# Storing sums of squares as rows, and the tail's results without a step's delay, in a hybrid attention encoder layer

## The chip, the cores and the metric

The kernel runs on one core of a Trainium2 chip. The metric is the device time in microseconds. The profiled execution is one more run of the same program, recorded by the hardware profiler.

## The reference

One layer of a bidirectional encoder is applied to two request groups of 2048 tokens each, with model width 1024, in float32. Both share one set of weights:

```python
h = rms_norm(x, norm_w)
proj = h @ w_in          # [q_a 512 | k_a 128 | v_a 128 | g_a 512 | q_b 512 | k_b 512 | v_b 512 | g_b 512]
...
o_a = windowed_gqa_sink(q_a, k_a, v_a, sink_a) * jax.nn.silu(g_a)
...
o_b = neighbourhood_attn(q_b, k_b, v_b, rpb_b) * jax.nn.silu(g_b)
x = x + jnp.concatenate([o_a, o_b], axis=-1) @ w_out
gate = jax.nn.sigmoid(x @ w_ple_gate)
return x + (p @ w_ple) * gate
```

Group A is attention within 128 tokens on either side, 8 query heads over 2 key heads, with normalised and partly rotated q and k and a learned sink. Group B is attention over a grid 64 tokens wide, in windows of 8 by 16, with a learned relative bias. `rms_norm` divides each row by the root of its mean square: the kernel works these means out once per row and uses them in both groups. The last two lines are the layer's tail: `p @ w_ple`, 256 inputs wide, can be computed at any time, since it needs nothing of the attention.

## The kernel before, in words

Matrices are held as a high and a low part, and each product is three matmuls of TensorE (PE). A sequence of 2048 rows is cut into NT = 16 blocks of 128. The stages follow each other in one stream:

- Stage A, f = 0 to 31, one step for each block of both sequences: `proj_a(f)` projects into pk, pq and pg (keys and values, queries, gate), while the two attention units of an earlier block run between its matmuls, at shares of the step that a table (PLAN_A) gives. In an attention unit, pt are transposes of the weights pr, po is the product with vv, and `fin` copies po with ACT (L738), adds with DVE (L741), multiplies by the gate pgt with DVE (L742) into ot and stores ot (L743, oa_d).
- Stage B, f = 32 to 95, the same for group B in two halves of the heads: the matmuls are pqk and pvg, with weight blocks wa and wb that are loaded when a half begins (L192).
- `ple_ahead(n)` computes `p @ w_ple` for n = 0 to 7, 512 columns each, in eight results m = 0 to 7 (pple, six matmuls each). Five of them (AHEAD) run inside the stream beside the last attention units, and n = 5, 6, 7 run as the tail behind it. ACT copies each result into a tile ev (L1007), and SP stores that to ple_d[n] (ple_d_327, 328 and 329 are those of n = 5, 6 and 7), from where it is read at the very end.
- The output projection and the gate's product, in seven products a step (acca, accc), each with operands opd that ACT and DVE split from loaded blocks raw (L1158, L1160), combined weights s (L1140) and residual blocks xres (L1245).

All large DMAs are issued by SyncE (SP), in order. A scheduler orders the instructions of each engine by when their inputs and buffers are free; those in `P(...)` or `pinned(...)` keep the order of the program. PSUM has three sets of buffers: "pj" with 3, "sc" with 3 and "ms" with 2; po, pqt (transposes of q) and the small transposes share "ms". In the tail, ev has five buffers (tag "s", SB = 5).

The means of squares of block f stand in column f of ms_a, one per partition. Stage B needs them in another order, as rows of the grid, in ms_b. So `proj_a` stores each column to DRAM:

```python
P(nc.sync.dma_start(ms_d[128 * f:128 * f + 128].rearrange("(p c) -> p c", c=1), ms))
```

This is L601: 128 pieces of one number. After the last block of a sequence (t == NT-1, so f = 15 and 31) `regroup(s)` lists the 16 reads of ms_b from ms_d (L639), which are issued two at a time from then on, and `stats_b(s)` works on ms_b later. Loads of the next rows are stn (normalised path, L338, read by ACT's squares at L369) and stx.

In `ple_ahead`, a store is put on a list and asked for when the next result has been copied, so always one result later:

```python
P(nc.scalar.copy(ev, ps))
store_ple(1)
made.append((ple_d[n][:, m], ev))
```

`load_coming()` asks for the next of eight weight blocks that the output product needs (wb, L976).

Of the kernel before, what the change touches and what calls it, by code (L numbers as in the profile page):

```python
# [11 lines left out]
F32 = mybir.dt.float32  # L12
# [5 lines left out]
SEQ = 2048  # L18
DM = 1024
NT = SEQ // 128  # L20
# [80 lines left out]
def emit(ctx, tc, io):  # L101
    nc = tc.nc
# [4 lines left out]
    def ptile(shape, tag, name):  # L107
        tag = PSM.get(tag, tag)
        return pp.tile(shape, F32, tag=tag, name=name, bufs=PSB[tag])
# [8 lines left out]
    ms_a = cp.tile([128, 2 * NT], F32, tag="ms_a", name="ms_a")  # L118
# [11 lines left out]
    ms_d = dram.tile([2 * SEQ], F32, tag="ms_d", name="ms_d")  # L130
# [28 lines left out]
    P = tc.keep_in_program_order  # L159
# [6 lines left out]
    def flush(key):  # L166
        pump(max((i + 1 for i, (k, _) in enumerate(jobs) if k == key), default=0))
# [72 lines left out]
    def pinned(ins):  # L240

        if last_pe:
            tc.add_manual_dep(ins.ins, last_pe.pop().name,
                              mybir.DependencyInfo(mybir.DependencyClass.NoSync, mybir.DependencyReason.DATA),
                              reason="tensor engine order")
        last_pe.append(ins.ins)
# [7 lines left out]
    def mm(out, lhsT, rhs, start, stop):  # L254
        pinned(nc.tensor.matmul(out, lhsT, rhs, start=start, stop=stop))  # L255

    def tr(out, in_, eye=ident):
        pinned(nc.tensor.transpose(out, in_, eye))  # L258
# [63 lines left out]
    ap = ab_stack.enter_context(tc.tile_pool(name="ab", bufs=1))  # L322
# [60 lines left out]
    ps = ptile([128, 512], "ms", "pwarm")  # L383
# [82 lines left out]
    for i in range(2):  # L466
        t = ap.tile([128, 2, 512], F32R, tag=f"q2{i}", name=f"q2{i}")
# [24 lines left out]
    def proj_a(f):  # L492
        s, t = divmod(f, NT)
# [68 lines left out]
        sq = ap.tile([128, 512], F32, tag="sq", name="sq", bufs=2)  # L562
# [35 lines left out]
        else:  # L598
            gate()
        held[f] = q, gs, y  # L600
        P(nc.sync.dma_start(ms_d[128 * f:128 * f + 128].rearrange("(p c) -> p c", c=1), ms))  # L601
        if t == NT - 1:
            regroup(s)
        else:
            regroup_next()
# [23 lines left out]
    def regroup(s):  # L629
        rows = ms_d.rearrange("(r k c) -> r k c", k=4, c=16)  # L630
        regroups.extend((ms_b[:, i:i + 1], rows[8 * (i // 4):8 * (i // 4) + 8, i % 4, :].rearrange("r c -> c r"))
                        for i in range(NT * s, NT * s + NT))
# [3 lines left out]
    def regroup_next():  # L636

        for dst, src in regroups[:2]:
            P(nc.sync.dma_start(dst, src))  # L639
        del regroups[:2]  # L640
# [293 lines left out]
    ple_d = [dram.tile([128, KT, TW], F32, tag=f"ple_d{n}", name=f"ple_d{n}") for n in range(len(tiles))]  # L934
    p_st, p_rs, early = {}, {}, {}

    def load_p(n):
        if n < len(tiles):
            s, u = tiles[n]
            p_st[n] = []  # L940
            for k in range(2):
                st = main.tile([128, TW], F32, tag="stage", name="p32", bufs=2)
                nc.sync.dma_start(st, io["p_t"][s][128 * k:128 * k + 128, TW * u:TW * u + TW])
                p_st[n].append(st)

    def split_p(n, later=False):

        t = p_rs[n] = main.tile([128, 2, 2, TW], F32R, tag="xr", name="p_r", bufs=2)

        def job(hi, lo, src):  # L950
            nc.scalar.copy(hi, src)
            nc.vector.tensor_tensor(out=lo, in0=src, in1=hi.bitcast(F32), op=ALU.subtract)
        for k, src in enumerate(p_st.pop(n)):
            todo = partial(job, t[:, k, 0], t[:, k, 1], src)
            if later:
                jobs.append((f"p{n}", todo))
            else:
                todo()
# [13 lines left out]
    def load_coming(n=1):  # L972

        for name, tag, key in coming[:n]:
            w = main.tile([128, 2, 512], F32R, tag=tag, name=tag, bufs=1)
            nc.sync.dma_start(w.bitcast(F32), parts_d[key])  # L976
            early[name].append(w)
        del coming[:n]

    made = []  # L980

    def store_ple(n):

        for dst, ev in made[:n]:
            nc.sync.dma_start(dst, ev)
        del made[:n]

    def ple_ahead(n, tail=False):

        load_p(n + 1)  # L990
        for m in range(KT):
            if m % 4 == 3 and (n < 3 or m == 3):
                load_coming()
            ps = ptile([128, TW], "pj", "pple")
            if m == 5 and n + 1 < len(tiles):
                split_p(n + 1)
            flush("p0")
            for k in range(2):
                w, c = early["p"][2 * (m // 4) + k], 128 * (m % 4)
                for i, (a, b) in enumerate(((0, 0), (0, 1), (1, 0))):  # L1000
                    mm(ps, w[:, a, c:c + 128], p_rs[n][:, k, b], k == 0 and i == 0, k == 1 and i == 2)
                    yield 215
            if tail:
                ev = main.tile([128, TW], F32, tag="s", name="ev", bufs=SB)
            else:
                ev = ap.tile([128, TW], F32, tag=("ev", "sq")[m // 2 % 2], name="ev", bufs=3 - m // 2 % 2)
            P(nc.scalar.copy(ev, ps))  # L1007
            store_ple(1)
            made.append((ple_d[n][:, m], ev))

    qs = {}

# [4 lines left out]
    def filler(f):  # L1017

        gen = proj_a(f) if f < 2 * NT else proj_b(f)
        for n, (cost, last_one) in enumerate(gen):  # L1020
            if last_one:
                next(gen)
            elif hold[0] > 0:
                hold[0] -= 1
            elif n % step[0] == step[0] - 1:
                pump()
            yield cost

    def drain(gen, count=10 ** 9):
        for _ in range(count):  # L1030
            if next(gen, None) is None:
                return
# [16 lines left out]
    def paired(f, n):  # L1049
# [20 lines left out]
        else:  # L1070
            for name in ("a12", "a22"):
                load_early(name)
        w_b[half] = w

    stream = chain(*(paired(f, last[f]) if f in last else filler(f) for f in range(2, 6 * NT) if f - 1 not in last),
                   *(ple_ahead(n) for n in range(AHEAD)))
    drain(stream, 24)
    done = 2
# [32 lines left out]
                keys_b(*p)  # L1111
            owed = 16
    drain(stream)
    store_ple(1)


    ab_stack.close()
    with tc.tile_pool(name="c", bufs=1, reuse_waits="tile") as op:
# [171 lines left out]

        load_raw(0, 0)
        drain(ple_ahead(AHEAD, True))
        load_raw(0, 1)
        drain(ple_ahead(AHEAD + 1, True))
        for _ in range(4):
            load_x()
# [5 lines left out]
            piece(0, k)  # L1302
        load_q(0, "s2")
        drain(rest)
        store_ple(1)
        for _ in range(4):
            load_x()
        for name in ("s1", "s3", "s4"):
# [1 line left out]
        for m in range(7 * len(groups)):  # L1310
            n, i = divmod(m, 7)
# [92 lines left out]
```

## Time and profile before

| | |
|---|---|
| time, median of 3 runs | 2491.75 us (2488.02 to 2493.52) |
| profiled execution | 2489.69 us, span 2487.9 us, mean granted TensorE clock 0.997 |
| busy time in the span | PE 2459.3, PEld 2078.0, DVE 1702.9, ACT 1413.9, POOL 863.4 us |
| ms_d stores | 32, of 0.5 KB each, in 128 pieces |
| HBM traffic | 308.24 MB read, 133.19 MB written, 177 GB/s over the span |

PE is TensorE's matmuls, PEld its weight loads (beside the matmuls), DVE the vector engine, ACT the scalar engine, POOL GpSimd and SPq the DMA queue of SyncE. An engine's row counts its own work, not its waits. The granted clock is TensorE's, 1.00 being full speed.

### The profile page before, as it was taken

How to read it: one execution, taken by the hardware profiler on the slowest of the kernel's cores; microseconds unless marked ns; L12 is line 12 of the kernel's file. 1: busy time of each engine (PE TensorE's matmuls, PEld its weight loads, DVE VectorE, ACT ScalarE, POOL GpSimd, SP SyncE). 2: the span in 40 equal slices, each digit the busy share in tenths (PEclk: the TensorE clock that was granted, in tenths of full speed). 3: DMA queues.
4: the chain of work that ended last, by engine and by line, in shares of the span. 5: the costliest groups of instructions: out<-in, count | busy, mean ns of one | idle time of the engine just before them, and what ended most of it. 6: DMA issues, size and time to landing. Idle time of an engine off the chain costs nothing.

```text
span 2487.9 us, 40537 instructions
## 1 busy us (share of the span) xinstructions
PE 2459.3 (99%) x13048; PEld 2078.0 (84%) x13048; DVE 1702.9 (68%) x4210; ACT 1413.9 (57%) x3405; POOL 863.4 (35%) x1365
## 2 busy tenths in 40 slices
PE   9999999999999999999999999999999999999999
PEld 7888888888878888888788888888777888888887
DVE  6777777777765666666666666666536655687776
ACT  6777776777664665565656566666653222344443
POOL 5555555555444544544444444443100000000000
PEclk9999999999999999999999999999999999999999
DMA  7655554455374566555855566667876445756765
GB/s 204 143 111 96 98 88 102 96 92 98 82 195 137 167 190 183 169 167 184 288 171 184 177 205 210 199 198 239 295 255 233 161 169 175 267 171 219 243 227 169
DMA packets 247140, 438.87 MB, mean 176 GB/s; under 512 B 32400, under 2 KB 86800, under 8 KB 241680
## 3 DMA queue, kind: packets, MB, share of 16 engines
q1 hardware_dynamic: 246640, 436.27, 59.6%
q8 instruction: 104, 1.70, 0.3%
q14 instruction: 108, 0.88, 0.1%
q10 hardware_dynamic: 288, 0.01, 0.0%
HBM read 308.24 MB, written 133.19 MB: 177 GB/s over the span
## 4 chain that ended last, share of the span: by engine, by line
PE 91%; DMA 4%; DVE 3%; ACT 1%; issue 1%; POOL 0%; SPq 0%; ACTq 0%; DVEq 0%; POOLq 0%
PE pqk L255 14%; PE acca L1226 14%; PE pvg L255 14%; PE accc L1226 10%; PE pg L255 6%; PE pq L255 5%; PE scb L255 4%; PE ptb L258 3%; PE pob L255 3%; PE pple L255 3%; PE pk L255 3%; PE po L255 3%; PE sc L255 3%; PE pt L258 2%; DMA stn<-x_n 1%; DMA vw<-v_d 1%
## 5 line engine op out<-in xcount | busy, mean ns | idle before, releaser
L287 ACT ACTIVATE s<-s,nm 128x320 f32<-128x320 f32 (+6 forms) x512 | 294.4, 576 | 314.9 <-DVE nm L282 193.9
L255 PE MATMUL pvg<-wb,xr 128*128 128x512 f32 x1536 | 462.6, 408 | 1.3 <-DMA wb<-sp_0wb 0.6
L255 PE MATMUL pqk<-wa,xr 128*128 128x512 f32 x1536 | 442.9, 410 | 0.0
L255 PEld LDWEIGHTS pqk<-wa,xr 128*128 128x128 f32 x1536 | 266.1, 189 | 36.9
L255 PEld LDWEIGHTS pvg<-wb,xr 128*128 128x128 f32 x1536 | 266.7, 189 | 34.2 <-DMA wb<-sp_0wb 2.2
L1208 ACT CAST opd<-raw 128x512 fp32r<-128x512 f32 x224 | 131.5, 618 | 273.3 <-PE acca L1226 115.2
L356 POOL TENSOR_TENSOR xr<-stx,xr 128x512 fp32r<-128x512 f32 x188 | 241.6, 1295 | 106.3 <-ACT xr L355 84.0
L1209 DVE TENSOR_TENSOR opd<-raw,opd 128x512 fp32r<-128x512 f32 x224 | 146.4, 685 | 151.7 <-ACT opd L1208 151.7
L255 PE MATMUL pg<-wb,xr 128*128 128x512 f32 x768 | 233.5, 410 | 1.8 <-DVE vv L518 1.0
L255 PE MATMUL pq<-wa,xr 128*128 128x512 f32 x768 | 219.4, 400 | 0.0
L271 DVE CUSTOM_DVE_ANT_0 s<-scb,bias 128x288 f32<-128x288 f32 (+3 forms) x256 | 142.0, 555 | 104.6 <-PE scb L255 104.5
L137 POOL TENSOR_TENSOR yb<-vrb,power 128x8 f32<-128x8 f32 x64 | 106.5, 1664 | 236.1 <-DVE vrb L787 222.6
L1226 PE MATMUL accc<-opd,wb 128*128 128x512 f32 x768 | 176.7, 389 | 0.0
L1226 PE MATMUL acca<-opd,wa 128*128 128x512 f32 x768 | 176.6, 391 | 0.0
L1226 PE MATMUL acca<-opd,s 128*128 128x512 f32 x768 | 175.4, 389 | 0.0
L1226 PEld LDWEIGHTS acca<-opd,wa 128*128 128x128 f32 x768 | 145.1, 189 | 30.3
L1226 PEld LDWEIGHTS accc<-opd,wb 128*128 128x128 f32 x768 | 144.2, 188 | 29.9
L1226 PEld LDWEIGHTS acca<-opd,s 128*128 128x128 f32 x768 | 144.2, 188 | 29.9
L918 DVE TENSOR_TENSOR otb<-pob,otb 64x512 f32<-64x512 f32 x128 | 88.1, 689 | 112.8 <-ACT otb L917 111.2
L255 PEld LDWEIGHTS pob<-p_t,vw 128*128 128x128 f32 (+2 forms) x832 | 133.0, 189 | 27.6 <-DVE p_t L899 5.0
L255 PEld LDWEIGHTS pq<-wa,xr 128*128 128x128 f32 x768 | 135.1, 189 | 17.3
L715 DVE TENSOR_TENSOR pr<-pt,pr 128x512 fp32r<-128x512 f32 (+2 forms) x248 | 135.5, 549 | 16.5 <-ACT pr L713 13.2
(167 smaller groups left out, 5177.0 us busy)
## 6 DMA issues: line engine op xcount, KB each, us to landing
stx<-x_b SPq DMA_DIRECT2D x128, 256.0 KB
vw<-v_d SPq DMA_DIRECT2D x112, 256.0 KB
stx<-x_a SPq DMA_DIRECT2D x64, 256.0 KB
stn<-x_n SPq DMA_DIRECT2D x64, 256.0 KB
v_d<-vb SPq DMA_DIRECT2D x64, 256.0 KB
ple_d<-ev SPq DMA_DIRECT2D x64, 256.0 KB
xres<-x_r SPq DMA_DIRECT2D x64, 256.0 KB
x_d<-r SPq DMA_DIRECT2D x64, 256.0 KB
```

The lines of the kernel that those rows point to most:

```text
L137: nc.gpsimd.tensor_tensor(out=y, in0=v, in1=power.broadcast_to([128, n]), op=ALU.pow)
L255: pinned(nc.tensor.matmul(out, lhsT, rhs, start=start, stop=stop))
L258: pinned(nc.tensor.transpose(out, in_, eye))
L271: nc.vector.tensor_tensor_reduce(out=s, in0=ps[:, :n], in1=bias, scale=1.0, scalar=-3.0e38, op0=ALU.add, op1=ALU.max, accum_out=sm["mx"][: ...
L287: ex = nc.scalar.activation(ss[i], ss[i], AF.Exp, bias=nm[:, i:i + 1], accum_out=den[:, i:i + 1])
L356: low.tensor_tensor(out=lo, in0=raw, in1=hi.bitcast(F32), op=ALU.subtract)
L715: nc.vector.tensor_tensor(out=pr[r, 1, to], in0=pt[r, c], in1=pr[r, 0, to].bitcast(F32), op=ALU.subtract)
L918: nc.vector.tensor_tensor(out=ot[a:a + 64], in0=pq[a:a + 64], in1=ot[a:a + 64], op=ALU.add)
L1208: P(nc.scalar.copy(hi, v))
L1209: P(nc.vector.tensor_tensor(out=lo, in0=v, in1=hi.bitcast(F32), op=ALU.subtract))
L1226: pinned(nc.tensor.matmul(ps, w[k][:, a, c:c + 128], o[:, b], start=i in (0, 1, 4) and k == 0 and j == 0, stop=k == 3 and j == 2, skip_gro ...
```

## The change

It has three parts.

1. The 32 stores of ms_d columns are gone. At f = 15 and f = 31, after pg's matmuls and the gate, PE transposes the sequence's 16 columns of ms_a into a PSUM tile pms (tag "ms", 16 x 128), ACT copies it to a tile row, and SP stores 16 rows of 128 numbers, 512 bytes each, in one DMA.
2. `ple_ahead` asks for one of the eight weight blocks per n, at m == 3, instead of two at n = 0, 1, 2 and one at n = 3, 4.
3. In the tail (n = 5, 6, 7) a result's store is asked for right after its copy, and the two `store_ple(1)` that stored what was left on the list are gone.

```diff
--- before.py
+++ after.py
@@ -598,8 +598,12 @@
         else:
             gate()
         held[f] = q, gs, y
-        P(nc.sync.dma_start(ms_d[128 * f:128 * f + 128].rearrange("(p c) -> p c", c=1), ms))
         if t == NT - 1:
+            ps = ptile([128, 512], "ms", "pms")
+            tr(ps[:NT, :128], ms_a[:, NT * s:NT * s + NT])
+            row = ap.tile([128, 512], F32, tag="sq", name="row", bufs=2)
+            P(nc.scalar.copy(row[:NT, :128], ps[:NT, :128]))
+            P(nc.sync.dma_start(ms_d[s * SEQ:(s + 1) * SEQ].rearrange("(t p) -> t p", p=128), row[:NT, :128]))
             regroup(s)
         else:
             regroup_next()
@@ -989,7 +993,7 @@
 
         load_p(n + 1)
         for m in range(KT):
-            if m % 4 == 3 and (n < 3 or m == 3):
+            if m == 3:
                 load_coming()
             ps = ptile([128, TW], "pj", "pple")
             if m == 5 and n + 1 < len(tiles):
@@ -1006,7 +1010,10 @@
                 ev = ap.tile([128, TW], F32, tag=("ev", "sq")[m // 2 % 2], name="ev", bufs=3 - m // 2 % 2)
             P(nc.scalar.copy(ev, ps))
             store_ple(1)
-            made.append((ple_d[n][:, m], ev))
+            if tail:
+                nc.sync.dma_start(ple_d[n][:, m], ev)
+            else:
+                made.append((ple_d[n][:, m], ev))
 
     qs = {}
 
@@ -1111,7 +1118,6 @@
                 keys_b(*p)
             owed = 16
     drain(stream)
-    store_ple(1)
 
 
     ab_stack.close()
@@ -1302,7 +1308,6 @@
             piece(0, k)
         load_q(0, "s2")
         drain(rest)
-        store_ple(1)
         for _ in range(4):
             load_x()
         for name in ("s1", "s3", "s4"):
```

PE at the end of stage A (f = 31), where pg's last matmuls are followed by stage B's first (pqk) and by the transposes of the gate (pgt) and of q (pqt); before:

```order
2815 L255 MATMUL pg<-wb_120,xr 128x512 x3
2816 L255 MATMUL pqk<-wa_9639,xr 128x512 [waits DMAHW0_49]
2817 L255 MATMUL po<-pr,vv 128x512 [waits Activation_49]
2818 L255 MATMUL po<-pr,vv 128x512
2819 L255 MATMUL pqk<-wa_9639,xr 128x512
2820 L255 MATMUL pqk<-wa_9639,xr 128x512 [waits Pool_49]
2821 L255 MATMUL pqk<-wa_9641,xr 128x512 [waits DMAHW1_49]
2822 L255 MATMUL pqk<-wa_9641,xr 128x512
2823 L258 MATMUL pgt<-ident,g_9740 128x128 [waits DVE_49]
2824 L258 MATMUL pgt<-ident,g_9740 128x128
2825 L258 MATMUL pqt<-ident,q 128x2x64 [waits PE_49]
```

and now:

```order
2816 L255 MATMUL pg<-wb_120,xr 128x512 x3
2817 L258 MATMUL pms<-ident,ms_a 16x128 [waits PE_49]
2818 L255 MATMUL pqk<-wa_9614,xr 128x512 [waits DMAHW3_49]
2819 L255 MATMUL po<-pr,vv 128x512 [waits Activation_49]
2820 L255 MATMUL po<-pr,vv 128x512
2821 L255 MATMUL pqk<-wa_9614,xr 128x512
2822 L255 MATMUL pqk<-wa_9614,xr 128x512 [waits Pool_49]
2823 L255 MATMUL pqk<-wa_9616,xr 128x512 [waits DMAHW4_49]
2824 L255 MATMUL pqk<-wa_9616,xr 128x512
2825 L258 MATMUL pgt<-ident,g_9715 128x128 [waits DVE_49]
2826 L258 MATMUL pgt<-ident,g_9715 128x128
2827 L258 MATMUL pqt<-ident,q 128x2x64 [waits Activation_49]
```

One transpose of ms_a stands behind pg, and pqt waits for ACT where it waited for PE itself. At f = 15 the same transpose stands between the last pg and the first pk of f = 16, and waits for DVE, PE and ACT.

SP at the same place; wb are the weight blocks of stage B's first half, stx rows of x, oa_d group A's results. Before:

```order
242 L743 DMA oa_d_84<-ot 128x2x128
243 L601 DMA ms_d<-ms_a 128x1
244 L192 DMA wb_9859<-sp_0wb_188 128x1024
245 L338 DMA stx<-x_b 128x512 x2
246 L601 DMA ms_d<-ms_a 128x1
247 L192 DMA wb_9861<-sp_0wb_189 128x1024
248 L192 DMA wb_9863<-sp_0wb_190 128x1024
249 L192 DMA wb_9865<-sp_0wb_191 128x1024
250 L192 DMA wb_9867<-sp_0wb_192 128x1024
251 L192 DMA wb_9869<-sp_0wb_193 128x1024
252 L192 DMA wb_9871<-sp_0wb_194 128x1024
253 L192 DMA wb_9873<-sp_0wb_195 128x1024
```

and now:

```order
215 L747 DMA oa_d_84<-ot 128x2x128
216 L192 DMA wb_9837<-sp_0wb_188 128x1024
217 L338 DMA stx<-x_b 128x512 x2
218 L192 DMA wb_9839<-sp_0wb_189 128x1024
219 L192 DMA wb_9841<-sp_0wb_190 128x1024
220 L192 DMA wb_9843<-sp_0wb_191 128x1024
221 L192 DMA wb_9845<-sp_0wb_192 128x1024
222 L192 DMA wb_9847<-sp_0wb_193 128x1024
223 L606 DMA ms_d<-row 16x128
224 L192 DMA wb_9849<-sp_0wb_194 128x1024
225 L192 DMA wb_9851<-sp_0wb_195 128x1024
226 L643 DMA ms_b<-ms_d 128x1x1 x2
```

The two stores of one column are gone, one store of 16 rows stands ahead of the last two wb, and the reads of ms_b follow it.

SP in the tail, where the stores of n = 6 (ple_d_328) and n = 7 (ple_d_329) meet the loads of the output product. Before:

```order
889 L985 DMA ple_d_328<-ev 128x512 x7
890 L1245 DMA xres<-x_r 128x512 x4
891 L1158 DMA raw<-oa_d_83 128x4x512
892 L1160 DMA raw<-ob_d_85 128x2048
893 L985 DMA ple_d_328<-ev 128x512
894 L985 DMA ple_d_329<-ev 128x512 x2
895 L1140 DMA s_23454<-sums_228 128x512
896 L1140 DMA s_23456<-sums_228 128x512
897 L1140 DMA s_23458<-sums_228 128x512
898 L1140 DMA s_23460<-sums_228 128x512
899 L985 DMA ple_d_329<-ev 128x512 x6
900 L1245 DMA xres<-x_r 128x512 x4
```

and now:

```order
860 L1014 DMA ple_d_328<-ev 128x512 x6
861 L1146 DMA s_23433<-sums_228 128x512
862 L1014 DMA ple_d_328<-ev 128x512
863 L1146 DMA s_23435<-sums_228 128x512
864 L1014 DMA ple_d_328<-ev 128x512
865 L1251 DMA xres<-x_r 128x512 x4
866 L1164 DMA raw<-oa_d_83 128x4x512
867 L1166 DMA raw<-ob_d_85 128x2048
868 L1014 DMA ple_d_329<-ev 128x512 x3
869 L1146 DMA s_23437<-sums_228 128x512
870 L1146 DMA s_23439<-sums_228 128x512
871 L1014 DMA ple_d_329<-ev 128x512 x5
```

The last store of n = 6 has moved ahead of the loads xres and raw, and two of the four s loads stand further up. The eight loads of part 2 stand between the same neighbours in both.

## The prediction

> **What bounds the kernel now.** I read the page first, then the waits of PE, a table of windows round the longest of them, the timelines of the queue and engines there, and the chain that ended last.
>
> ```profile
> span 2487.9 us, 40537 instructions
> ...
> PE 2459.3 (99%) x13048; PEld 2078.0 (84%) x13048; DVE 1702.9 (68%) x4210; ACT 1413.9 (57%) x3405; POOL 863.4 (35%) x1365
> ```
>
> PE is busy for 2459.3 of 2487.9 us. The change takes no matmul away, so it can win only idle PE time, plus time in which PE ran at half clock. The waits of PE (engine, tile and line that waited, releaser; us in total, times, longest) say where the idle time lies:
>
> ```profile
> PE pple L255 <- ACT ev L1007: 5.7, 1, 5.7
> PE pt L258 <- DVE ot L742: 5.4, 2, 4.9
> ...
> PE pvg L255 <- DMA wb<-sp_0wb: 0.6, 2, 0.3
> ```
>
> Two single waits stand out, 5.7 us in the tail and 4.9 us at the end of group A's projections. The windows (stretch; length, then busy time of PE, PEld, DVE, ACT, POOL; granted clock, DMA share, GB/s) cover both:
>
> ```profile
> 667.00:674.00 7.00, 7.00 (x43) 6.00 (x42) 2.84 (x13) 2.39 (x9) 4.58 (x13) 1.00 0.50 20
> 674.00:679.00 5.00, 0.47 (x5) 0.26 (x3) 1.23 (x4) 3.30 (x10) 0.00 (x0) 0.98 0.51 172
> 679.00:682.00 3.00, 2.65 (x13) 2.65 (x14) 2.88 (x7) 2.05 (x5) 0.00 (x0) 0.50 0.21 68
> 704.00:713.00 9.00, 9.00 (x52) 7.77 (x51) 6.16 (x18) 5.17 (x15) 4.52 (x7) 1.00 0.95 44
> 1770.00:1774.40 4.40, 2.50 (x14) 1.72 (x13) 1.53 (x4) 1.94 (x5) 1.15 (x3) 1.00 1.07 314
> 1774.50:1777.80 3.30, 3.30 (x11) 2.73 (x10) 0.91 (x2) 1.47 (x3) 0.00 (x0) 0.50 0.96 358
> 1862.50:1868.50 6.00, 0.37 (x2) 0.00 (x0) 1.39 (x2) 0.59 (x2) 0.00 (x0) 0.84 1.02 399
> 1868.50:1873.40 4.90, 4.85 (x11) 3.80 (x12) 0.00 (x0) 1.87 (x4) 0.00 (x0) 0.50 0.99 378
> ```
>
> Each idle stretch is followed by a stretch at granted clock 0.50: 2.65 us of PE work after the first, 4.85 us after the second. The DMA column differs between the two places: in the tail the queues move 399 GB/s and are full, at 667 they are half busy and move 20 GB/s.
>
> **Part 1, the sums of squares.** What stands in SP's queue before that slow stretch is a per-block store of 128 single numbers, then the load of the next block's rows, stn:
>
> ```profile
> 662.75 0.80 SPq L601 DMA_DIRECT2D ms_d<-ms_a  x1
> ...
> 666.34 1.58 SPq L338 DMA_DIRECT2D stn<-x_n  x2
> ```
>
> The chain that ended last has that load, and one of the same kind early on, beside a load of the same shape (stx) that had no such store ahead of it (start, duration, what):
>
> ```profile
> 38.99 2.72 DMA stx<-x_a
> ...
> 43.75 9.09 DMA stn<-x_n
> ...
> 666.34 9.18 DMA stn<-x_n
> ```
>
> A clean landing takes 2.72 us, one behind the store 9.18 us. Then ACT, in order, waits with its squares for stn, and everything queued behind it waits too, among it the copy that PE's transposes need:
>
> ```profile
> 675.60 0.63 ACT L369 ACTIVATE stn<-stn 128x512 f32<-128x512 f32 x1 [4.92 <-DMA stn<-x_n]
> ```
> ```profile
> 679.35 0.69 PE L258 MATMUL pt<-ident,s 128*128 128x128 f32 x2 [4.88 <-DVE ot L742]
> ```
>
> ACT was free at 675.60 − 4.92 = 670.68. With a clean landing stn is there at 666.34 + 1.58 + 2.72 = 670.6 at the latest, so ACT starts 4.92 us sooner and PE's transposes come at 679.35 − 4.92 = 674.43, just where PE's idle time began (679.35 − 4.88 = 674.47). The stall goes whole: 4.88 us. The half-clock stretch behind it goes with it: half of 2.65, 1.3 us. The windows have a second clogged place, 704 to 713: share 0.95 at 44 GB/s with the last two of these stores in the queue ahead of the eight weight blocks wb. The two waits of pvg for wb, 0.6 us, are put down to it. Other late stn loads on the chain (43.75) left no long wait of their own on PE; they are taken at nothing. Gain: 4.88 + 1.3 + 0.6 = 6.8 us.
>
> The Trainium skill, "DMA: Bandwidth & Descriptors", section "Anatomy of one DMA — SWDGE (gpsimd) path", gives a transfer a fixed cost of about 2.0 us and then its bytes; by that alone a store of 512 bytes would have been gone at 664.8 and would hold nothing, and this part would win nothing, as in rival (b). The same page's "Specifications" say that pieces under 512 bytes cost a read-modify-write, which agrees with the 20 GB/s and speaks the other way.
>
> What is added are two transposes on PE, two small ACT copies, and two stores of 16 rows in the place of 32. The transpose of f=15 needs the PSUM buffer of po, which DVE gives back with the second of these:
>
> ```profile
> 348.97 0.86 DVE L741 TENSOR_TENSOR ot<-po,ot 64x256 f32<-64x256 f32 x2 [2.17 <-ACT ot L738]
> ```
> ```profile
> 349.28 1.37 PE L255 MATMUL pk<-wx,xr 128*128 128x256 f32 x10
> ```
>
> It stands on PE ahead of these matmuls, so PE waits from 349.28 to 349.83: 0.6 us, and the matmuls of pk and all of the next block stand behind it. At f=31 the new transpose itself finds its buffer free, but the four transposes of q behind it now take the same buffer after the row's copy, which comes on ACT after the gate's tanh:
>
> ```profile
> 713.45 0.69 ACT L592 ACTIVATE gs<-pg,y 128x512 f32<-128x512 f32 x1
> ```
> ```profile
> 713.55 0.60 PE L258 MATMUL pqt<-ident,q 128*128 128x128 f32 x4
> ```
>
> No row of before copies 16x128. It lies between a 128x4 and a 128x128 operation of ACT:
>
> ```profile
> 713.23 0.19 ACT L293 ACTIVATE es<-es 128x4 f32<-128x4 f32 x1
> ```
> ```profile
> 665.04 0.28 ACT L506 ACTIVATE sq<-pk 128x128 f32<-128x128 f32 x1
> ```
>
> I take the latter, as it is the nearer in width. tanh ends at 714.14, the copy at 714.42, so PE waits 0.9 to 1.0 us instead of starting at 713.55. Cost: 0.6 + 1.0 = 1.6 us, from 0 (if the work behind catches up at a later wait) to 1.6 plus a half-clock stretch for each (below). On SP the row's store of f=31 waits for that copy too, until about 714.5, with the last two wb blocks, two loads of ms_b and an oa_d store queued behind it; the wb blocks overwrite what pg's matmuls read until about 713, and with the clog gone they land before pvg wants them. Part 1 together: −6.8 + 1.6 = −5.2 us.
>
> **Part 2, the weight blocks.** In program order the eight loads are spread over eight row blocks instead of five. The order of SP's queue has them between the same neighbours as before, since the scheduler places them by when their buffers come free. Nothing removed, nothing added: 0 us. The clock loss at 1774 (rows above) stays, as it follows waits for vw.
>
> **Part 3, the tail's stores.** Before, each result's store was asked for one product later, so the last one of 328 stood behind the loads for the output products:
>
> ```profile
> 1853.29 3.30 SPq L1245 DMA_DIRECT2D xres<-x_r  x4
> 1856.64 0.43 SPq L1158 DMA_DIRECT2D raw<-oa_d  x1
> 1857.12 0.50 SPq L1160 DMA_DIRECT2D raw<-ob_d  x1
> 1857.72 2.05 SPq L985 DMA_DIRECT2D ple_d<-ev  x3
> ```
>
> Its data had been ready since 1853.41 + 0.59 = 1854.0:
>
> ```profile
> 1853.41 0.59 ACT L1007 COPY ev<-pple 128x512 f32<-128x512 f32 x1 [0.55 <-PE pple L255]
> ```
>
> The chain and the two engines show what the place cost: the store landed 10.09 us after its issue, ACT's next copy waited for that ev buffer, and PE for the copy.
>
> ```profile
> 1857.72 10.09 DMA ple_d<-ev
> ```
> ```profile
> 1867.91 1.56 ACT L1007 COPY ev<-pple 128x512 f32<-128x512 f32 x3 [7.25 <-DMA ple_d<-ev]
> ```
> ```profile
> 1868.55 2.93 PE L255 MATMUL pple<-p_r,wa 128*128 128x512 f32 x6 [5.68 <-ACT ev L1007]
> 1871.28 2.32 PE L1226 MATMUL acca<-opd,wa 128*128 128x512 f32 x5
> ```
>
> After, this store is issued at once, ahead of those 3 MB, and can land before the copy wants its buffer (1867.91 − 7.25 = 1860.7), even at several times the clean 2.72 us. PE then runs its last product without the 5.68 us, and the 4.85 us of work at clock 0.50 shrink by half, 2.4 us. Late next is the following ev buffer: its store now goes out behind the raws and lands at about 1867, but what needs the PSUM behind it is only the third accumulator of the output product, since the first two sit in other buffers; so I take nothing for it. The loads pushed back by one store lose under 1 us of a full queue, and the operands' splitting has the time that the last 5.68 us gave back. Gain: 5.68 + 2.4 = 8.1 us.
>
> **The sum.** −5.2 + 0 − 8.1 = −13.3 us. The profiled execution took 2489.69 us (1.8 us beyond its span), which gives 2476.4. It lies 2.06 us under the median of the three runs (2488.02 to 2493.52); the mean of all four times is 2490.75, and from there the forecast is 2477.4 us.
>
> **Rivals.** (a) Only part 1 wins. The tail's queue is full (399 GB/s at 1862 to 1868), so the wait moves to the next ev buffer or to the output product's operands and is paid in the same size. Against it is the buffer order above; for it, that the same bytes have to pass. Time: 2490.75 − 5.2 = 2485.5. (b) Only part 3 wins. What holds stn may not be the 4-byte store: half a KB could be gone well inside the 2.72 us that a clean load of 256 KB takes, that is before 666.34, and then stn is late for another reason that the change leaves as it is. For it, the slow stretch lasts to 674, over 11 us after the store's issue; against it, the clean load and the late ones differ in nothing else that the trace shows. The costs of the two transposes stay: 2490.75 + 1.6 − 8.1 = 2484.2. (c) Slower: the two new waits of PE come on PE's path at 349 and 713, and each also trips the clock, while (a) and (b) both fail. In the windows 1.9 us of idle PE time within 4.40 us (1770) was followed by 3.30 us at 0.50, a loss of 1.65 us; it decides from about that much idle time in one such stretch, and the new waits are put at 0.6 and 1.0. Price 1.6 + 2 × 1.65 = 4.9: 2495.6. The Trainium skill, "TensorE: Matmul & The Clock Gate", Part 1's table of the two states, has the clock drop only after an idle window of about 3.4 us, by which (c) would cost 1.6 us at most; the 1770 row, where it dropped after 1.9 us of scattered idleness, differs from that. (d) Both wins are nothing and the costs hidden: 2490.8, for instance if the stall at 674 returns because the next load is late and the tail is bound by bytes.
>
> **How the numbers follow.** Both parts win 0.62 (2477.4), (a) 0.12, (b) 0.12, (c) 0.07, (d) 0.07. A measurement of this kernel tells about 0.2%, 5 us, from no change. (a) and (b) lie near that edge and are split two to one: faster 0.62 + 0.16 = 0.78, within 0.2% 0.08 + 0.07 = 0.15, slower 0.07. The lower end takes the new costs as hidden (−1.6), and the best of the runs shown (2488.02, 2.7 under the mean) with some of the late early loads won as well: 2471. The upper end reaches over (a) and (b) to 2487; (c) and (d) are left out.
>
> **What would show it.** In the profile after: PE's wait of pt for ot at 674 gone and no clock of 0.50 at 679; stn landing in about 3 us; a small PE wait at pk of f=16 and at pqt of f=31; no ACT wait of 7 us for ple_d at 1860 and no PE wait at pple. A wait of acca or accc in the first 15 us of the output products would speak for (a), a slow stn with no ms_d store ahead of it for (b), a clock of 0.50 at 350 or 715 for (c). The forecast is wrong if the time does not fall by more than 5 us.

## The result, and the profile after

The change took 2474.14 us (median of six runs, 2473.60 to 2477.33) where the kernel before took 2492.64 us (median of six, 2488.02 to 2497.40): a ratio of 0.9928, 95% interval 0.9915 to 0.9941, that is 18 us less, 15 to 21. The profiled pair went from 2489.69 to 2477.33 us, 12.4 us less. The kernel before spreads more from run to run than the change does; what that means for the sum comes below.

The page of the change, its first part:

```profile
span 2475.5 us, 40506 instructions
...
PE 2455.8 (99%) x13050; PEld 2074.9 (84%) x13050; DVE 1704.6 (69%) x4210; ACT 1413.6 (57%) x3407; POOL 863.3 (35%) x1365
```

PE's busy time fell by 3.5 us and its idle time by 8.9 us. Of the two waits of PE (us in total, times, longest) that headed the table before, that of pple for ev is gone, and that of pt for ot is down from 5.4 us to 0.6. The longest is now the wait of group B's product (pob) for its loaded values vw, ahead of the tail. It was 2.6 us in all before, and neither part 1 nor part 3 touches it. Two small new ones belong to the added transposes:

```profile
PE pob L255 <- DMA vw<-v_d: 4.2, 4, 2.6
...
PE pqt L258 <- ACT row L605: 0.5, 1, 0.5
PE pms L258 <- DVE ot L745: 0.5, 1, 0.5
```

At the end of stage A, SP's timeline has no ms_d store ahead of stn. The second of the two stn loads stands in the chain that ended last, with 4.37 us where the first of them had 9.18 before. That is more than the 2.72 us of a clean load, but ACT's squares start without a wait for it:

```profile
662.76 0.38 SPq L747 DMA_DIRECT2D oa_d<-ot  x1
666.77 1.59 SPq L338 DMA_DIRECT2D stn<-x_n  x2
```
```profile
668.03 4.37 DMA stn<-x_n
```
```profile
671.03 0.62 ACT L369 ACTIVATE stn<-stn 128x512 f32<-128x512 f32 x1
```

The windows answer to those of before (length; busy PE, PEld, DVE, ACT, POOL; granted clock, DMA share, GB/s):

```profile
667.00:674.00 7.00, 7.00 (x42) 5.98 (x40) 3.44 (x15) 4.48 (x16) 5.04 (x13) 1.00 0.38 116
674.00:677.00 3.00, 2.42 (x22) 2.22 (x20) 2.86 (x9) 2.91 (x8) 0.00 (x0) 1.00 0.42 131
704.00:713.00 9.00, 8.48 (x47) 7.03 (x47) 5.66 (x16) 5.57 (x16) 2.70 (x5) 1.00 0.95 337
1860.00:1862.50 2.50, 2.50 (x13) 2.07 (x12) 0.69 (x1) 0.00 (x0) 0.00 (x0) 1.00 1.06 425
1862.50:1868.50 6.00, 6.00 (x28) 4.99 (x27) 2.15 (x4) 3.78 (x8) 0.00 (x0) 1.00 1.03 398
```

In the stretch from 704 to 713 the DMA engines are as busy as before, 0.95, but move 337 GB/s in place of 44. In the tail they are as full as before, 398 against 399 GB/s, yet PE is busy for all 6.00 us where it was busy for 0.37. No clock of 0.50 is left in these rows.

The tail on SP, ACT and PE: the last store of n = 6 is issued at 1850.98, ahead of the loads. ACT still waits for an ev buffer, 7.40 us, but one result later, and PE runs through from the last pple to acca.

```profile
1850.98 0.41 SPq L1014 DMA_DIRECT2D ple_d<-ev  x1
1851.48 2.06 SPq L1251 DMA_DIRECT2D xres<-x_r  x4
1854.19 0.38 SPq L1164 DMA_DIRECT2D raw<-oa_d  x1
1854.84 0.33 SPq L1166 DMA_DIRECT2D raw<-ob_d  x1
```
```profile
1864.64 1.85 ACT L1011 COPY ev<-pple 128x512 f32<-128x512 f32 x3 [7.40 <-DMA ple_d<-ev]
```
```profile
1839.74 20.57 PE L255 MATMUL pple<-p_r,wa 128*128 128x512 f32 x89
1860.15 11.04 PE L1232 MATMUL acca<-opd,wa 128*128 128x512 f32 x48
```

### The profile page after: what moved, and what is told of

Its sections match the earlier page's. It is cut to its first block, busy times and chain, and to the rows that moved or that the text cites. A ratio compares the mean times of both kernels' runs of the same rounds, so it can differ in the third digit from the quotient of the medians.

```text
span 2475.5 us, 40506 instructions
## 1 busy us (share of the span) xinstructions
PE 2455.8 (99%) x13050; PEld 2074.9 (84%) x13050; DVE 1704.6 (69%) x4210; ACT 1413.6 (57%) x3407; POOL 863.3 (35%) x1365
## 4 chain that ended last, share of the span: by engine, by line
PE 92%; DVE 3%; DMA 2%; ACT 2%; POOL 1%; issue 1%; SPq 0%; DVEq 0%; ACTq 0%; POOLq 0%
PE pqk L255 14%; PE acca L1232 14%; PE pvg L255 14%; PE accc L1232 10%; PE pg L255 6%; PE pq L255 6%; PE scb L255 4%; PE ptb L258 3%; PE pk L255 3%; PE pob L255 3%; PE pple L255 3%; PE po L255 3%; PE sc L255 3%; PE pt L258 2%; DMA vw<-v_d 1%; DVE pr L719 1%
```

## The experiments

Each experiment was timed in turns with the kernel before on its chip. That kernel's medians were 2489.55 us beside the first four, 2490.21 beside the next four and 2489.35 beside the last three.

### Each part alone

Part 1 alone is the diff's block in `proj_a`, part 2 alone its condition in `ple_ahead`, part 3 alone the direct store and the two calls that it makes needless. A fourth kernel has one line more than the kernel before:

```diff
         drain(ple_ahead(AHEAD + 1, True))
+        store_ple(1)
         for _ in range(4):
             load_x()
```

> Only part 1 (row stores). Theory: the stall of pt for ot at 674, its half-clock stretch and the wb waits go, two small waits are added, so 5 us less in the profiled execution (-4 to -6) and no PE wait of over 1.5 us at the end of stage A; the tail keeps its 5.7 us wait. Rival 1: the stores are not what holds stn, then +1 to +2 us and the wait at 674 stays. Rival 2: the 5 to 6 us by which the timed runs of the change win more than the profiled pair (18.5 against 12.4) come from part 1, whose stall then differs from run to run: 9 to 12 us less.

> Only part 3 (tail stores asked for at once). Theory: the 5.7 us wait of pple and its half-clock stretch go, 8 us less (-7 to -9), the stage A stall stays. Rival 1: the wait returns at acca or accc, 0 to 2 us less. Rival 2: the extra 5 to 6 us of the timed runs come from the tail: 13 us less.

> The kernel before with one line more: the last result of n = 6 is stored ahead of the loads xres and raw, all other tail stores stay one result late. Theory: this one store carries all of part 3, 8 us less, within 1 us of the direct stores. Rival: storing each result a step sooner is what matters, since the queue is full; then 0 to 4 us less and an ACT wait for ev stays on PE's path.

> Only part 2 (one weight block asked for per row block). Theory: SP's queue has the eight loads between the same neighbours, so no change, within 1 us of before. Rival: the small shifts in the queue ease the vw waits at 1770 and win 1 to 3 us, or make them longer by as much.

| | median, us | ratio to before, 95% interval | difference, us |
|---|---|---|---|
| part 1, rows | 2483.56 | 0.9975 (0.9966 to 0.9984) | −6.2 (−8.5 to −4.0) |
| part 3, direct stores | 2481.68 | 0.9971 (0.9959 to 0.9982) | −7.2 (−10.2 to −4.5) |
| one store moved | 2482.96 | 0.9975 (0.9965 to 0.9985) | −6.2 (−8.7 to −3.7) |
| part 2, weight blocks | 2490.19 | 1.0002 (0.9993 to 1.0011) | +0.5 (−1.7 to +2.7) |

The last column is the ratio applied to the 2489.55 us of the kernel before; it differs by up to 0.7 us from the difference of the two medians. Parts 1 and 3 each took away their own wait and left the other's. The longest wait of PE in the profiles of part 1 alone, part 3 alone and the one store moved, in this order:

```profile
PE pple L255 <- ACT ev L1011: 4.6, 1, 4.6
```
```profile
PE pt L258 <- DVE ot L742: 4.3, 1, 4.3
```
```profile
PE pt L258 <- DVE ot L742: 4.7, 1, 4.7
```

Rivals (a) and (b) of the prediction fall with this, since both parts win. The one store wins as much as all direct stores within the intervals, so part 3's gain hangs on the place of one store of 256 KB ahead of 3 MB of loads. Part 2 is nothing that can be measured.

### Whether the parts add up

> The whole change once more, beside the others on one chip. If its parts add up, it wins what they won alone, 6.2 + 7.2 + 0 = 13 us. If there is something between the parts, it wins 18 us again, 5 more than their sum.

The change once more: 2475.20 us (2473.91 to 2476.37), ratio 0.9944 (0.9930 to 0.9957), 13.9 us less (10.7 to 17.4). The parts alone sum to 12.9 (6.2 + 7.2 − 0.5), so nothing between them shows; the intervals reach some 3 us to either side, and less than that could hide in them. The 18 us of the first comparison go back to the kernel before: its median was 2492.64 there and 2489.35 to 2490.21 in the three others, while the change took 2474.14 there and 2475.20 here. Why before took some 3 us more in that first one is left open.

### What held the load of stn

The change gets its per-block stores back, at their old place, into a scratch buffer that nobody reads. In the first kernel each is 128 pieces of one number, in the second one piece of 512 bytes, in the third 128 pieces again, but issued by ACT:

```diff
+        P(nc.sync.dma_start(ms_x[128 * f:128 * f + 128].rearrange("(p c) -> p c", c=1), ms))           # pieces
+        P(nc.sync.dma_start(ms_x[128 * f:128 * f + 128].rearrange("(p c) -> p c", p=1), ident[0:1, :]))  # whole
+        P(nc.scalar.dma_start(ms_x[128 * f:128 * f + 128].rearrange("(p c) -> p c", c=1), ms))         # pieces, ACT
         if t == NT - 1:
```

> The whole change, with the per-block stores of 128 single numbers put back at their old place, into a scratch buffer that nobody reads; the results still come from the row stores. Theory (these small pieces hold up the load of stn behind them): stn lands in 8 to 10 us again, the PE wait at 674 comes back, 4 to 6 us slower than the change alone. Rival (what held stn was something else, for instance the wait of SP for the column or the order of the queue): within 1 us of the change.

> The same as the run before, but each scratch store is one piece of 512 bytes from one partition in the place of 128 pieces of 4 bytes. Theory: the number of pieces costs, not the store: stn lands in 3 to 4.5 us and the time is within 1 us of the change alone. Rival: any store at that place holds the load, 4 to 6 us slower.

> The whole change, with the per-block scratch stores of 128 single numbers issued by ACT in the place of SP, so that they stand in another queue than the load of stn. If the pieces hold the DMA engines that all queues share, stn is late again and the time is 4 to 7 us over the change (2475.2). If they hold only what stands behind them in SP's own queue, stn lands in 3 to 4.5 us and the time is within 1.5 us of the change.

| | median, us | lowest to highest | over the change (2475.20) |
|---|---|---|---|
| pieces of 4 bytes, SP | 2482.43 | 2480.97 to 2483.57 | +7.2 |
| one piece of 512 bytes, SP | 2474.92 | 2473.55 to 2476.27 | −0.3 |
| pieces of 4 bytes, ACT | 2496.32 | 2493.64 to 2499.46 | +21.1 |

The 7.2 us of the first kernel lie above the 4 to 6 that were expected, and near the 6.8 that the prediction puts on these stores alone: this kernel, too, pays for the two transposes. The third ran beside a kernel before of 2489.35 us, 0.9 us under that of the other two, which is small against its 21 us.

With the pieces on SP, the load of stn in the chain and PE's wait are back where they were, and so are the slow windows:

```profile
666.90 8.92 DMA stn<-x_n
```
```profile
PE pt L259 <- DVE ot L748: 5.8, 3, 4.5
```
```profile
667.00:675.00 8.00, 8.00 (x48) 6.79 (x46) 3.40 (x14) 2.39 (x9) 5.12 (x13) 1.00 0.43 34
704.00:713.00 9.00, 9.00 (x54) 7.71 (x53) 6.41 (x18) 5.17 (x15) 4.83 (x8) 1.00 0.91 50
```

The same windows with the same store in one piece:

```profile
667.00:675.00 8.00, 8.00 (x52) 7.00 (x51) 5.17 (x19) 6.84 (x22) 4.26 (x13) 1.00 0.44 139
704.00:713.00 9.00, 8.49 (x48) 6.90 (x47) 5.26 (x15) 5.97 (x17) 3.99 (x7) 1.00 0.97 358
```

34 and 50 GB/s became 139 and 358 with as many bytes stored at the same place. The one-piece store reads a row that is ready early (ident) and not the column of the block, but that is not the difference: SP issued either store 0.43 us after the store of oa_d and 3.6 us ahead of stn. So it is the cutting into 128 pieces of 4 bytes that costs. It is not their number alone: the store of oa_d just ahead, which the change has too, went out as 256 pieces of 512 bytes, and stn landed in 4.37 us behind it. Whether the size of a piece counts, or that all 128 go into the same 512 bytes of memory, these runs do not separate.

How such pieces slow a load is open too, since they do not stand in its way for long. In the trace of the first kernel each of them took 9 ns at most, and the last was over at 665.2, ahead of the issue of stn at 666.90. What is long are packets of the load itself: of the 256 packets of 2 KB of the two stn loads, 14 took over 1 us and the longest 6.39 us; with the store in one piece none took over 0.6 us.

By the fixed 2.0 us plus bytes of the Trainium skill ("DMA: Bandwidth & Descriptors", "Anatomy of one DMA — SWDGE (gpsimd) path") both stores would have been the same; the two runs differ by 7.5 us. The Trainium skill states that fit for another path than these DMAs, which SP and ACT issue.

On ACT's queue the pieces did not spare SP's loads. The third kernel's timeline of ACT's queue, its chain and a window between them show the first two such stores and the loads that SP issued just behind them:

```profile
32.13 0.34 ACTq L602 DMA_DIRECT2D ms_x<-ms_a  x1
...
44.08 0.33 ACTq L602 DMA_DIRECT2D ms_x<-ms_a  x1
```
```profile
33.59 9.59 DMA stn<-x_n
...
45.24 10.32 DMA stx<-x_a
```
```profile
32.50:39.50 7.00, 7.00 (x41) 5.98 (x40) 3.77 (x7) 2.17 (x5) 4.50 (x9) 1.00 0.89 20
```

The loads land 9.6 and 10.3 us after their issue, from a queue in which no such store stands (in before, the second of the same two stn loads landed in 2.83 us): the pieces hold something that the queues share. The extra time is larger than on SP, and most of it, about 15 us by the start of PE's matmuls, lies in the first 60 us. There ACT waits 8.02 and 6.70 us for these two loads, and PE has the longest wait of each of these two rows:

```profile
PE sc L256 <- DVE mx L272: 9.6, 3, 9.2
PE sc L256 <- POOL q L318: 3.9, 1, 3.9
```

From 47 to 60 us the granted clock was 0.50 as well. With the stores on SP, the first two went out at 22.90 and 41.06 and no such wait of PE came of them. The expectation of 4 to 7 us had the direction and not the size: it took the place of the stores for given.

### Weight blocks really moved, and the transposes without a wait

In the first kernel part 2's loads are pinned in program order. The second also asks for them later, two, three and three at n = 2, 3 and 4:

```diff
-            if m == 3:
+            if m in {2: (3, 7), 3: (1, 4, 7), 4: (1, 4, 7)}.get(n, ()):
                 load_coming()
...
-            nc.sync.dma_start(w.bitcast(F32), parts_d[key])
+            load = nc.sync.dma_start(w.bitcast(F32), parts_d[key])
+            if tag[1] == "b":
+                P(load)
```

The third adds to this that ms_a is transposed into the free half of pkt, the PSUM tile of the block's transposed keys, and copied from there:

```diff
-        pkt = ptile([128, 128], "ms", "pkt")
+        pkt = ptile([128, 256], "ms", "pkt")
...
+        if t == NT - 1:
+            tr(pkt[:NT, 128:], ms_a[:, NT * s:NT * s + NT])
```

> The whole change, with the loads of part 2 pinned in program order, so that one weight block really is asked for per row block, the last three of them in the tail. By the theory that part 2 did nothing because the scheduler moved the loads back up, this is what it would do if it held: the vw waits shrink (2 to 3 us won), but three blocks of 0.5 MB enter the tail, whose queue is full; at 360 GB/s they cost 4 us there, so 0 to 3 us over the change, with an ACT wait for ev or a PE wait in the first products. Rival: the tail has room, 2 to 3 us under the change.

> The whole change, with the eight weight blocks really moved: pinned in program order and asked for two at n = 2, three at n = 3 and three at n = 4, so that they leave the stretch where PE waits for vw. Theory: the waits of pob for vw (4.2 us in all in the profile of the change) and a half-clock stretch behind them go, 3 to 6 us faster than the change alone. Rival 1: the loads only move the crowd, and vw waits come at 1800 or the wait for ev in the tail grows: within 1 us. Rival 2: they arrive late for the second product: slower by 2 us or more, with a wait of accc.

> The change with the weight blocks moved as in the run e10_later, and the transpose of ms_a put into the free half of the PSUM tile of the transposed keys (pkt), so that it takes no buffer of its own. Theory: the two new PE waits (0.5 and 0.5 us in the profile of the change) go, 1 us under e10_later (2472.2), that is 2471. Rival: what waits behind them waits later anyway, no difference.

Pinned: 2473.69 us (2473.43 to 2475.06), ratio 0.9938 (0.9926 to 0.9951). Later: 2472.19 us (2472.16 to 2473.76), 0.9933 (0.9920 to 0.9945). With the shared tile: 2471.72 us (2471.08 to 2475.22), 0.9932 (0.9919 to 0.9946). Moving the loads later beat the change by 3.0 us on the same chip, without overlap of the runs (the change's were 2473.91 to 2476.37). PE's waits for vw, the change's in the same comparison first, then those with the loads later:

```profile
PE pob L255 <- DMA vw<-v_d: 2.7, 2, 2.4
```
```profile
PE pob L255 <- DMA vw<-v_d: 1.4, 2, 0.9
```

The windows at this place, for the same two profiles in the same order, show a half-clock stretch as well, which the later loads do not have (length, busy PE; granted clock third from the end):

```profile
1760.00:1770.00 10.00, 7.53 (x36) 5.72 (x35) 3.45 (x8) 5.33 (x16) 2.43 (x5) 0.88 1.03 321
1770.00:1780.00 10.00, 10.00 (x54) 8.42 (x54) 5.31 (x16) 7.00 (x18) 0.73 (x1) 0.95 0.65 211
```
```profile
1760.00:1770.00 10.00, 10.00 (x57) 8.26 (x56) 4.59 (x10) 8.04 (x21) 2.43 (x5) 1.00 0.96 303
```

But the first profile of the change had these waits without that stretch:

```profile
1760.00:1770.00 10.00, 7.30 (x41) 5.58 (x39) 4.16 (x11) 6.47 (x18) 2.44 (x5) 1.00 1.01 333
1770.00:1780.00 10.00, 9.67 (x54) 8.31 (x55) 4.81 (x14) 5.72 (x13) 0.00 (x0) 1.00 0.80 265
```

The place varies that much between profiles of one kernel, so that the 3.0 us come from there is likely, and not shown. The pinned kernel ran on another chip than the change. By its ratio to before it cannot be told from the change; a loss of up to 3 us, as expected, does not show. Whether the shared tile wins anything over the later loads cannot be told from the times: 0.5 us lies inside either's runs. In its profile both new PE waits are gone.

## Why the prediction was right

The forecast, 2477.4 us in a range of 2471 to 2487, had the sign, both places and the mechanism. By its steps:

- **The stall at 674.** Forecast 4.88 us. PE's wait of pt for ot went from 4.88 to 0.57 us (first row of the change below), so 4.3 us. In the second profile of the change it is gone.
- **The half-clock stretch behind it.** Forecast 1.3 us. This is the term that was mis-sized most. PE's timeline of before, then of the change, from the same four transposes to the fourth pair of sc:

```profile
679.35 1.12 PE L258 MATMUL pt<-ident,s 128*128 128x128 f32 x4 [4.88 <-DVE ot L742]
680.12 2.24 PE L255 MATMUL pk<-wx,xr 128*128 128x256 f32 x9
682.18 0.47 PE L255 MATMUL sc<-ks_a,q 128*128 128x320 f32 x2
...
683.78 0.45 PE L255 MATMUL sc<-ks_a,q 128*128 128x320 f32 x2
```
```profile
675.50 0.66 PE L258 MATMUL pt<-ident,s 128*128 128x128 f32 x4 [0.57 <-DVE ot L746]
675.92 1.31 PE L255 MATMUL pk<-wx,xr 128*128 128x256 f32 x9
677.07 0.45 PE L255 MATMUL sc<-ks_a,q 128*128 128x320 f32 x2
...
678.45 0.56 PE L255 MATMUL sc<-ks_a,q 128*128 128x320 f32 x2 [0.58 <-DVE pr L719]
...
679.82 0.46 PE L255 MATMUL sc<-ks_a,q 128*128 128x320 f32 x2
```

  Up to the first sc it takes 1.57 us in the place of 2.83: the clock's 1.26 us are won. From there to the fourth pair it takes 2.75 in the place of 1.60, with a wait for DVE that was not there, so only 0.1 us is left. In before, DVE was busy for 2.88 of the 3.00 us from 679 to 682; a faster PE only meets DVE sooner, and the step took half of the stretch as won without asking what else was full in it.
- **The weight blocks' clog (704 to 713).** Forecast 0.6 us from two waits of pvg for wb, which are gone from PE's table; the stretch now moves 337 GB/s. The gain there was larger than these waits, 1.5 to 1.6 us (table below).
- **The two added transposes.** Forecast 0.6 and 0.9 to 1.0 us; PE waited 0.47 us at f = 15 and 0.52 at f = 31, and with the transposes themselves the matmuls behind start 0.8 and 0.9 us later (table below), as forecast. The row's copy took 0.24 us, between the bounds of 0.19 and 0.28:

```profile
349.67 0.27 PE L258 MATMUL pms<-ident,ms_a 128*16 128x128 f32 x1 [0.47 <-DVE ot L745]
```
```profile
710.06 0.24 ACT L605 COPY row<-pms 16x128 f32<-16x128 f32 x1
```

  The windows behind them have the granted clock (third column from the end) at 1.00:

```profile
349.70:353.00 3.30, 3.30 (x30) 3.30 (x30) 2.63 (x7) 2.39 (x7) 1.74 (x6) 1.00 0.55 198
353.00:357.00 4.00, 4.00 (x27) 3.70 (x26) 3.90 (x15) 2.13 (x5) 3.65 (x4) 1.00 0.48 129
710.30:714.00 3.70, 3.65 (x20) 3.04 (x21) 3.41 (x6) 2.36 (x5) 2.06 (x3) 1.00 0.94 353
714.00:718.00 4.00, 4.00 (x23) 3.08 (x22) 2.55 (x7) 2.89 (x6) 3.15 (x7) 1.00 0.59 189
```

  So of rival (c) only the waits came, and no half-clock stretch behind them; they were a quarter of the 1.9 us from which it had decided. That figure is no threshold either: the first profile of the change had PE idle for 2.70 us between 1760 and 1770 and the clock stayed at 1.00 (rows above).
- **Part 1 together.** Forecast −5.2; −6.2 (−8.5 to −4.0) alone.
- **Part 2.** Forecast 0 from the queue's order; +0.5 (−1.7 to +2.7). That the clock loss at 1774 stays held for the second profile of the change and not for the first.
- **Part 3.** Forecast −8.1; −7.2 (−10.2 to −4.5) alone. That the next ev buffer would be late without costing anything came as stated: 7.40 us of ACT's wait lie beside a PE that does not stop. The list of signs said the opposite, no such wait of ACT, and was wrong there.
- **The sum.** Forecast −13.3. The profiled pair gave −12.4, the second comparison −13.9 (−17.4 to −10.7), the first −18. Rival (d) and the slower side fall.

The traces allow the terms to be measured one by one. If each matmul of PE is matched with the same one of before (the same tile, the same place in the count), the shift of its start says what was won up to there, and the difference of two shifts what was won between (us; negative is earlier than before):

| stretch, by the time in before | forecast | profile of the change | its second profile | the part alone |
|---|---|---|---|---|
| 347 to 351, transpose at f = 15 | +0.6 | +0.8 | +0.8 | +0.8 |
| 672 to 685, stall and half clock | −6.2 | −4.4 | −5.2 | −4.6 |
| 707 to 716, transpose at f = 31 | +1.0 | +0.9 | +0.9 | +0.9 |
| 718 to 745, weight blocks | −0.6 | −1.6 | −1.6 | −1.5 |
| 1858 to 1878, tail | −8.1 | −8.3 | −8.2 | −8.3 |

The one store moved also has −8.3 in the tail. The tail and the transposes were forecast to about 0.2 us. The stall with its half clock brought 1.0 to 1.8 us less than the sum has, and the weight blocks 1 us more: that the sum of part 1 came out is luck in these two terms. Where the 1 us more at the weight blocks comes from is open.

## What to carry to other kernels

A store of half a kilobyte can hold up the loads behind it if it is cut into single numbers, here to 9 us from issue to landing in the place of 2.7 to 4.4: look in the windows for a high DMA share at a low GB/s, and at what was issued just ahead of it, whichever queue it is in. In a full queue, look for the one small store that stands behind large loads and gives back a buffer that PE will need. When an idle stretch is followed by a half-clock one, ask which other engine is full in it before the clock's loss is counted as won; here 0.1 us of 1.26 was left.

## What had not been expected of the hardware

Stores in pieces of 4 bytes slowed loads issued from another engine's queue as much as those behind them in their own: 9.6 and 10.3 us to landing with the stores on ACT's queue, 8.92 us with them on SP's. The DMA share stayed at 0.89 while 20 GB/s were moved, so that column alone does not tell a full queue from a clogged one.

The clock did not follow the idle time of PE alone. At the waits for vw it fell to 0.50 in before, after 1.9 us of idle time within 4.4 us. In the first profile of the change it stayed at 1.00 behind waits of 2.61 and 0.42 us that lay between 1766.9 and 1770.4. What decides between the two is not shown here.
